# Products with diagonals of 1/rms for turning x, and changed orders and buffers around four stages of a decoder block

## The chip, the cores and the metric

The kernel runs on one core of a Trainium2 chip. The metric is the device time of one execution in microseconds (us), as the median of several runs.

## What is computed

The reference is a decoder block over 1024 positions with 1024 channels, all in float32. Its core is

```python
mod = einsum('bd,de->be', silu(c), w_ada) + b_ada
sh1, sc1, g1, sh2, sc2, g2 = split(mod, 6)
h = rmsnorm(x, norm1_g) * (1 + sc1) + sh1
cb, cc, cv, q, k, v, f_logit, ga, gb = split(h @ w_in, IN_OFFSETS)
ya = cb * causal_dwconv(cc * cv, conv_a_w)
yb = forgetting_attention(rmsnorm(q), rmsnorm(k), v, log_sigmoid(f_logit + b_f))
merged = sigmoid(ga) * (ya @ w_branch_a) + sigmoid(gb) * (yb @ w_branch_b)
x = x + g1 * (merged @ w_out)
h2 = rmsnorm(x, norm2_g) * (1 + sc2) + sh2
gate, val = split(causal_dwconv(h2 @ w_up, conv_ffn_w), 2)      # 2816 channels each
x = x + g2 * ((silu(gate) * val) @ w_down)
```

where `rmsnorm(x, g)` is `x * rsqrt(mean(x*x) + 1e-6) * g`.

## The kernel before

Each float32 operand of a large product is split into a high part and a low part (type fp32r), and a product is the sum of three products of parts. The high part is a copy on ACT, the low part a subtraction on VectorE (DVE) or GpSimd (POOL); `wsplit` (L93, L94) does so for weights. Stages of the network that allow it use Strassen's seven products of blocks in place of eight.

In nearly every stage the order of the instructions on each engine is written out by hand: an engine runs them in the order of the code, and a semaphore wait holds up all that stands behind it on the same engine. The stages are these, by the profile's clock.

- **Head and K pass**, 0 to 78 us. x comes in eight tiles `xts[j]` of 128 positions by 1024 channels. `x_square` sums the squares of a tile on DVE (L292) or ACT (L290), `x_scale` takes the root and multiplies the tile in place by 1/rms (L299), `x_turn` transposes it on PE in two groups of four 128x128 blocks (L306), each copied by ACT into `raw` (L312). Meanwhile rows of the small vectors (`rc` for c, `rv` for gains and biases) are loaded and turned, and the modulation vector is summed: `ada_mul` and `ada_chain` multiply loaded weight blocks `wa` by columns of silu(c) and add them up on DVE, `ada_sum` sums over partitions by a product with ones (L249). `h_tile` applies shift and scale and splits h into parts; `k_mm` makes the K projection, one of eight blocks `dd` of channels at a time, for all tokens. Per odd `dd` the next unit of weights is split.
- **V pass**, 78 to 143 us, and **q pass**, 143 to 201 us. One token (128 positions) after the other is projected. An event table `at(t, f)` hangs the other work on units of PE's work of some 0.7 us each: the norm of the queries (L496 the sums of squares, L501 the normalised queries `qn`, L509 their transposes, L516 and L519 their parts), further blocks of the modulation vector (`rest_mul`: L460 and L463 on DVE, L461 and L464 on ACT, L465 and L467 on POOL), and 16 sums of blocks of h for a later Strassen stage (`t_sum`, L585).
- **Convolution and gates** 201 to 460 us, **attention** 460 to 700, **branches and output projection** 700 to 800.
- **Up-projection**, 800 to 1200 us. The first three units `u0`, `u1`, `u2` are plain products (`plain(n, half)`, n being one of four blocks of a gate or a value); from `U[3]` on it is Strassen. Each unit is scaled, goes through the taps of its convolution and is multiplied out (`scale_g`, `scale_v`, `taps_g`, `silu`, `taps_v`, `ff`, `ff_out`). The Strassen units need sums of blocks of h2 in parts; the sum `T4` (L1481, L1487, made by `t_op(kk, 3, ...)`) is written over the block `B12`, which the plain units still read.
- **Down-projection**, 1200 to 1458 us: seven Strassen products, each over 11 steps of `st.mm(banks)` (L1984). When a product is done, `x_add` adds it to the output blocks (L2009), and finished blocks are turned back: `x_turn_out` has four transposes on PE into the product's own bank (L2020), a copy on ACT (L2026) and a store. One product finishes two blocks, so that two such turns use the same bank.

Of the kernel before, what the change touches and what calls it, by code (L numbers as in the profile page):

```python
# [8 lines left out]
F32 = mybir.dt.float32  # L9
F32R = mybir.dt.float32r  # L10
AF = mybir.ActivationFunctionType
ALU = mybir.AluOpType
# [4 lines left out]
P = 128  # L17
S = 1024
D = 1024
# [14 lines left out]
def tile_hybrid_block(  # L34
# [27 lines left out]
    mm = tensor.matmul  # L62
# [154 lines left out]
    def ada_mul(wa, ks=range(ND), acc=None):  # L217


        acc = acc or [ap.tile([P, 2, P], F32, tag=f"wacc{i}", name="wacc", bufs=1) for i in range(2)]  # L220
        for k in ks:
            a, src = acc[k % 2], wa[:, :, k, :]
            if k < 2:
                vector.tensor_scalar(out=a, in0=src, scalar1=cT[:, k : k + 1], scalar2=None, op0=ALU.mult)
            else:
                vector.scalar_tensor_tensor(out=a, in0=src, scalar=cT[:, k : k + 1], in1=a, op0=ALU.mult, op1=ALU.add)
        if k < ND - 1:
            return acc
        vector.tensor_tensor(out=acc[0], in0=acc[0], in1=acc[1], op=ALU.add)
        return acc[0]  # L230

    def ada_chain(wa, part):

        sums = hT[:, 256:512].rearrange("p (i m) -> p i m", i=2)
        for k in range(4 * part, 4 * part + 4):
            src, c1 = wa[:, :, k, :], cT[:, k : k + 1]
            if k == 0:
                vector.tensor_scalar(out=sums, in0=src, scalar1=c1, scalar2=None, op0=ALU.mult)
                continue
            out = sums  # L240
            if k == ND - 1:
                out = ap.tile([P, 2, P], F32, tag="wacc0", name="wacc", bufs=1)
            vector.scalar_tensor_tensor(out=out, in0=src, scalar=c1, in1=sums, op0=ALU.mult, op1=ALU.add)
        return out

# [42 lines left out]
    def x_square(j, eng):  # L288
        if eng is scalar:
            scalar.activation(accs[2 if j > 3 else 0], xts[j], AF.Square, accum_out=ms[:, j : j + 1])  # L290
        else:
            vector.tensor_tensor_reduce(out=accs[2 if j > 3 else 1], in0=xts[j], in1=xts[j], scale=1.0, scalar=0.0,  # L292
                                        op0=ALU.mult, op1=ALU.add, accum_out=ms[:, j : j + 1])

    def x_scale(j, eng):
        js = slice(j, j + 1)
        vector.tensor_scalar(out=ms2[:, js], in0=ms[:, js], scalar1=1.0 / D, scalar2=EPS, op0=ALU.mult, op1=ALU.add)
        r = newton_rsqrt(xp, ms2[:, js], 1, "r1", root_of=(ms[:, js], 1.0 / D))
        eng.tensor_scalar(out=xts[j], in0=xts[j], scalar1=r, scalar2=0.0, op0=ALU.mult, op1=ALU.add)  # L299

    def x_turn(j, eng=scalar):
        for i in range(2):
            pt = aux_tile("xTp", ("aux", "aux2")[i])
            for n in range(4):
                dd = 4 * i + n
                tensor.transpose(pt[:, n * P : (n + 1) * P], xts[j][:, dd * P : (dd + 1) * P], ident)  # L306
            dst = raw[i, j // 4][:, :, (j % 4) * P : (j % 4 + 1) * P]
            src = pt.rearrange("p (a b) -> p a b", a=4)
            if i and eng is vector:
                vector.tensor_copy(dst, src)  # L310
            else:
                scalar.activation(dst, src, AF.Copy)  # L312
# [29 lines left out]

    scalar.activation(cT, rows_T(c_rows, "rc"), AF.Silu)
    x_square(0, vector)
    x_square(1, vector)
    x_scale(0, gpsimd)
    x_square(2, scalar)
    x_scale(1, vector)
    x_square(3, scalar)
    x_scale(2, gpsimd)  # L350
    x_turn(0)
    x_scale(3, vector)
    x_turn(1)
    vector.tensor_copy(vT[:, :76], rows_T(v_rows, "rv"))
    n1g, n2g = vT[:, 0:8], vT[:, 8:16]
    caw = vT[:, 16:28].rearrange("p (t n) -> p t n", t=3)
# [1 line left out]

    a1b = cp.tile([P, ND], F32, name="a1b")
    vector.scalar_tensor_tensor(out=a1b, in0=bada[:, 8:16], scalar=1.0, in1=n1g, op0=ALU.add, op1=ALU.mult)  # L360
    wc[0] = ada_mul(was[0])
    h_ada(3)
    x_turn(2)
    x_turn(3)
    units[0] = wsplit(kraw[0], gpsimd)
    h_mod(0, ada_sum(wc[0], aux_tile("pm")))
    h_tile(0, 0)
    for j in (4, 5):
        x_square(j, vector)
    for j in (4, 5):  # L370
        x_scale(j, gpsimd)
    for j in (6, 7):
        x_square(j, scalar)
    for j in (6, 7):
        x_scale(j, vector)
    k_mm(0, range(4))
    for j in range(4, NT):
        x_turn(j)
    acc0.append(aux_tile("k6", "aux2"))
# [9 lines left out]
    wc[2] = ada_chain(was[2], 1)  # L389
    h_ada(5)  # L390
    h_tile(1, 1)
    units[1] = wsplit(kraw[1], gpsimd)
    kraw[2] = unit_fetch(O_K, 512, 2)
    vraw = []
    for dd in range(1, ND):
        if dd == 2:
            kraw[3] = unit_fetch(O_K, 512, 3)
        if dd > 4:
            vraw.append(unit_fetch(O_V, 520, dd - 5))
        if dd == ND - 1:  # L400
            for j in range(7):
                for t in TERMS:
                    k_mm(dd, (j,), (t,))
            break
        k_mm(dd, range(7), TERMS[:1])
        if dd % 2:
            units[dd // 2 + 1] = wsplit(kraw[dd // 2 + 1], gpsimd)
        h_mod(dd + 1, ada_sum(wc[dd + 1], hT))
        if dd + 2 < ND:
            ada_chain(was[dd + 2], 0)  # L410
        h_tile(dd + 1, 0)
        if dd + 2 < ND:
            wc[dd + 2] = ada_chain(was[dd + 2], 1)
        if dd + 5 < ND:
            h_ada(dd + 5)
        h_tile(dd + 1, 1)
        k_mm(dd, range(7), TERMS[1:])
# [31 lines left out]
    def rest_mul(part):  # L449
# [2 lines left out]
            return  # L452
        b, wa = rest_open[0]
        if part == 0:
            rest_acc[:] = [ap.tile([P, 2, P], F32, tag=f"wacc{i}", name="wacc", bufs=1) for i in range(2)]
        even, odd = rest_acc
        k = 2 * part
        src, nxt = wa[:, :, k, :], wa[:, :, k + 1, :]
# [85 lines left out]
    def at(t, *fs):  # L544
        events.setdefault(t, []).extend(fs)
# [35 lines left out]

    def sub(o, a, b):
        gpsimd.tensor_tensor(out=o, in0=a, in1=b, op=ALU.subtract)  # L585

    def t_sum():

        kk, n = divmod(t_done.pop(0), 4)
        b11, b12, b21, b22 = (raw[i, g][:, kk] for i in range(2) for g in range(2))  # L590
        sub(*((b11, b12, b11), (b12, b22, b12), (b22, b22, b11), (b21, b21, b22))[n])

    t_done = list(range(16))

# [314 lines left out]
    at(TQ + 19, f_sum)  # L909
    at(TQ + 34, f_turn)  # L910
    for i in range(9):
        at(TQ + 8 * (i // 2) + (1, 3)[i % 2], t_sum)
    for i in range(4):
        at(TQ + (42, 45, 50, 53)[i], lambda i=i: t_split(T1, 0, 0, i, (vector, gpsimd)[i % 2]))
    at(TQ + 55, p0)
# [906 lines left out]
            U[3].fetch(up)  # L1822
    u2.xs = wsp[4:6]
    u2.g, u2.v = (acc4(nm) for nm in ("upg", "upv"))
    for n in (0, 2, 1, 3):
        for half in range(2):
            u2.plain(n, half)
    for kk in range(NK):
        t_op(kk, 3, False)
        t_op(kk, 3, True)  # L1830
    u1.scale_g()
    u1.scale_v()
    u1.taps_g()
    u1.silu()
    U[3].x_split()
    u1.taps_v()
    u1.ff()
    u1.ff_out()
# [211 lines left out]
    for t, st in enumerate(steps[: len(steps) - NE + 1]):  # L2050
# [28 lines left out]
            steps[t + 2].split()  # L2079
        for w in ends.get(t, ()):  # L2080
            w()
        while turns:
            x_turn_out(*turns.pop(0))
        if st.c > 0 and adds and (st.c % 2 == 0 or st.p == ORDER[-1]):
            adds.pop(0)()
        if t < len(steps) - NE:
            st.mm(banks)
    last = steps[-NE:]

    def finish(e):  # L2090
# [47 lines left out]
```

## Time and profile before

| | |
|---|---|
| time, three runs (us) | 1464.48, 1466.3, 1464.09; median 1464.48 |
| the profiled execution (us) | 1460.0 |
| its span, first to last instruction (us) | 1458.3 |
| mean granted clock of TensorE | 0.993 |
| PE busy | 1399.7 us, 96% |
| PE's weight loads (PEld) busy | 1154.3 us, 79% |
| DVE busy | 1086.3 us, 74% |
| ACT busy | 661.9 us, 45% |
| POOL busy | 515.2 us, 35% |

The profile is of one execution. PE stands for the matrix products, PEld for the loads of their stationary operand, which overlap them. Idle time of an engine is put down to the instruction on another engine, or the transfer, that ended it. Matmul ends are modelled, so PE's busy share is an upper bound. The granted clock is a share of full speed.

### The profile page before, as it was taken

To read this page: it belongs to the slowest core of one execution; us is meant where nothing else is said; L and a number is where in the kernel's file an instruction comes from. 1 tells how busy PE (TensorE), PEld (TensorE's weight loads), DVE (VectorE), ACT (ScalarE), POOL (GpSimd) and SP (SyncE) were. 2 spreads that over 40 slices of the span, in tenths; PEclk is the share of its full clock that TensorE was granted. 3 is DMA by queue.
4 is the path that set the end of the run, shared out by engine and by line. 5 is a ranking of instruction groups with operands and counts; after the bars stand their busy time and mean duration, and the time that the engine had idled before them with its cause. 6 is when DMAs were issued, how large, how long until landed. Compare 5 with 4: busy or idle time off the path is not lost. (4 is left out here: it accounts for less than half of the span.)

```text
span 1458.3 us, 19429 instructions
## 1 busy us (share of the span) xinstructions
PE 1399.7 (96%) x6680; PEld 1154.3 (79%) x6680; DVE 1086.3 (74%) x1779; ACT 661.9 (45%) x1147; POOL 515.2 (35%) x540
## 2 busy tenths in 40 slices
PE   5899899999999999999999989999999999999997
PEld 4688678887888888777788868888888887888876
DVE  7865588888777776448637867888887776898764
ACT  6554263434555555565225434544443334444443
POOL 2656457764555553323121013455543321000000
PEclk9999999999999999999999999999999999999999
DMA  9559434546555548676942223344322204983622
GB/s 287 164 165 312 131 101 118 158 110 202 152 145 144 145 123 280 219 258 230 201 131 73 72 69 103 89 116 116 101 87 88 87 29 143 388 290 104 215 77 78
DMA packets 260760, 222.45 MB, mean 153 GB/s; under 512 B 43117, under 2 KB 213445, under 8 KB 260661
## 3 DMA queue, kind: packets, MB, share of 16 engines
q1 hardware_dynamic: 259389, 218.61, 50.2%
q0 software_dynamic: 1136, 2.56, 0.6%
q8 instruction: 53, 0.87, 0.3%
q14 instruction: 46, 0.38, 0.1%
q10 hardware_dynamic: 136, 0.04, 0.0%
HBM read 169.76 MB, written 51.41 MB: 152 GB/s over the span
## 5 line engine op out<-in xcount | busy, mean ns | idle before, releaser
L1984 PE MATMUL dn<-bH,aH 128*128 128x512 f32 x308 | 120.9, 392 | 0.0
L1984 PE MATMUL dn<-bL,aH 128*128 128x512 f32 x308 | 120.2, 390 | 0.6 <-DVE bL L1978 0.6
L1984 PE MATMUL dn<-bH,aL 128*128 128x512 f32 x308 | 119.9, 389 | 0.0
L1594 ACT ACTIVATE wh<-ws 128x512 fp32r<-128x512 f32 x95 | 55.5, 626 | 119.8 <-POOL ws L1628 117.0
L753 DVE TENSOR_TENSOR ol<-ws,oh 128x512 fp32r<-128x512 f32 x98 | 92.5, 952 | 15.0 <-ACT oh L752 11.7
L94 DVE TENSOR_TENSOR wl<-ws,wh 128x1024 fp32r<-128x1024 f32 (+1 forms) x51 | 70.2, 1377 | 36.8 <-ACT wh L93 36.7
L752 ACT ACTIVATE oh<-ws 128x512 fp32r<-128x512 f32 x98 | 61.3, 627 | 70.7 <-PE pacc L798 36.9
L1628 POOL TENSOR_TENSOR ws<-ws 128x512 f32<-128x512 f32 x19 | 24.7, 1299 | 147.0 <-DVE wl L94 147.0
L1595 DVE TENSOR_TENSOR wl<-ws,wh 128x512 fp32r<-128x512 f32 x76 | 69.6, 935 | 8.9 <-ACT wh L1594 8.9
L1195 ACT ACTIVATE L<-L,mn 128x256 f32<-128x256 f32 (+6 forms) x56 | 46.4, 829 | 58.1 <-DVE mn L1193 56.6
L1198 POOL TENSOR_SCALAR L<-L,rs 128x384 f32<-128x384 f32 (+7 forms) x62 | 48.1, 776 | 68.4 <-DVE rs L1197 66.7
L1218 ACT ACTIVATE th<-pt 128x512 fp32r<-128x512 f32 (+1 forms) x80 | 43.9, 551 | 56.2 <-PE pt L1212 53.8
L1984 PEld LDWEIGHTS dn<-bL,aH 128*128 128x128 f32 x308 | 57.9, 188 | 13.2 <-DVE bL L1978 1.5
L585 POOL TENSOR_TENSOR ws<-ws 128x512 f32<-128x512 f32 x42 | 55.0, 1309 | 37.4 <-DVE ol L753 25.4
L1977 ACT ACTIVATE aH<-dws 128x512 fp32r<-128x512 f32 x52 | 32.8, 631 | 76.6 <-issue 44.1
L1984 PEld LDWEIGHTS dn<-bH,aH 128*128 128x128 f32 x308 | 57.8, 188 | 12.1 <-ACT bH L1977 0.4
L1984 PEld LDWEIGHTS dn<-bH,aL 128*128 128x128 f32 x308 | 57.8, 188 | 12.0
L93 ACT ACTIVATE wh<-ws 128x1024 fp32r<-128x1024 f32 (+1 forms) x58 | 60.9, 1052 | 11.2 <-PE k L556 3.1
L1219 DVE TENSOR_TENSOR tl<-pt,th 128x512 fp32r<-128x512 f32 (+1 forms) x80 | 50.5, 635 | 17.4 <-ACT th L1218 15.8
L1715 DVE SCALAR_TENSOR_TENSOR u<-upv,cwT,u 128x1023 f32<-128x1023 f32 (+1 forms) x44 | 56.4, 1281 | 9.5 <-ACT u L1711 8.8
L1595 POOL TENSOR_TENSOR wl<-ws,wh 128x512 fp32r<-128x512 f32 x19 | 24.6, 1297 | 109.3 <-ACT wh L1594 109.3
L1978 DVE TENSOR_TENSOR aL<-dws,aH 128x512 fp32r<-128x512 f32 x52 | 35.9, 691 | 36.3 <-ACT aH L1977 36.3
(571 smaller groups left out, 4523.1 us busy)
## 6 DMA issues: line engine op xcount, KB each, us to landing
wa<-in_w_ada_dram SPq DMA_DIRECT2D x48, 512.0 KB
dws<-in_w_down_dram SPq DMA_DIRECT2D x96, 256.0 KB
ws<-in_w_up_dram SPq DMA_DIRECT2D x44, 512.0 KB
ws<-in_w_in_dram SPq DMA_DIRECT2D x36, 512.0 KB
ff<-ff_d SPq DMA_DIRECT2D x44, 256.0 KB
ff_d<-u SPq DMA_DIRECT2D x21, 512.0 KB
xt<-in_x_dram SPq DMA_DIRECT2D x8, 512.0 KB
v_d<-vt SPq DMA_DIRECT2D x8, 512.0 KB
```

Of the source, the lines that this page charges most:

```text
L93: scalar.activation(wh[:, : n * m], ws[:, : n * m], AF.Copy)
L94: eng.tensor_tensor(out=wl[:, : n * m], in0=ws[:, : n * m], in1=f32(wh[:, : n * m]), op=ALU.subtract)
L585: gpsimd.tensor_tensor(out=o, in0=a, in1=b, op=ALU.subtract)
L752: scalar.activation(h, src, AF.Copy)
L753: eng.tensor_tensor(out=l, in0=src, in1=f32(h), op=ALU.subtract)
L1195: scalar.activation(L[:, :n], L[:, :n], AF.Exp, scale=-1.0, bias=mn, accum_out=sm)
L1198: eng.tensor_scalar(out=L[:, :n], in0=L[:, :n], scalar1=rs, scalar2=0.0, op0=ALU.mult, op1=ALU.add)
L1219: vector.tensor_tensor(out=flat[2][:, c0:], in0=flat[0][:, c0:], in1=f32(flat[1][:, c0:]), op=ALU.subtract)
L1594: scalar.activation(ops[0][:, sl], src, AF.Copy)
L1595: eng.tensor_tensor(out=ops[1][:, sl], in0=src, in1=f32(ops[0][:, sl]), op=ALU.subtract)
L1715: vector.scalar_tensor_tensor(out=u[:, s:], in0=acc[:, : S - s], scalar=cwT[:, 2 - s, n : n + 1], in1=u[:, s:], op0=ALU.mult, op1=ALU.add)
L1984: mm(banks[e], self.A[i][:, es_], self.B[j], start=self.p in FIRST and self.c == 0 and t == 0, stop=self.c == NC - 1 and t == 2, skip_grou ...
```

## The change

The roots are taken for two tiles at a time on DVE (`x_root`), which also makes for each tile a diagonal matrix of 1/rms, and `x_turn` multiplies each block of x by that diagonal in a plain float32 product in place of transposing a scaled block; `x_scale` is gone. The order of the head is rewritten around that: the small vectors' turn and copy come ahead of the second square, and the second four tiles' squares and roots come behind the first part of the K products. The low parts of the K weights move from POOL to DVE. The two accumulators of the modulation sums become one name with two buffers, and the odd sum is made in place in the loaded weights. Nine of the T sums of the q pass move from POOL to DVE. In the up-projection `u2`'s products have another order and T4's splits come behind `U[3].x_split()`. In the down-projection the second of two turns in one bank is placed between the two halves of the next step's products.

```diff
-        acc = acc or [ap.tile([P, 2, P], F32, tag=f"wacc{i}", name="wacc", bufs=1) for i in range(2)]
+        acc = acc or [ap.tile([P, 2, P], F32, tag="wacc", name="wacc", bufs=2), wa[:, :, 1, :]]
...
-                out = ap.tile([P, 2, P], F32, tag="wacc0", name="wacc", bufs=1)
+                out = ap.tile([P, 2, P], F32, tag="wacc", name="wacc", bufs=2)
...
-    def x_scale(j, eng):
-        js = slice(j, j + 1)
+    diags = {}
+    def x_root(j0):
+        js = slice(j0, j0 + 2)
         vector.tensor_scalar(out=ms2[:, js], in0=ms[:, js], scalar1=1.0 / D, scalar2=EPS, op0=ALU.mult, op1=ALU.add)
-        r = newton_rsqrt(xp, ms2[:, js], 1, "r1", root_of=(ms[:, js], 1.0 / D))
-        eng.tensor_scalar(out=xts[j], in0=xts[j], scalar1=r, scalar2=0.0, op0=ALU.mult, op1=ALU.add)
+        r = newton_rsqrt(xp, ms2[:, js], 2, "r1", root_of=(ms[:, js], 1.0 / D))
+        for i in range(2):
+            diags[j0 + i] = xp.tile([P, P], F32, tag="dg", name="dg", bufs=4)
+            vector.tensor_scalar(out=diags[j0 + i], in0=ident, scalar1=r[:, i : i + 1], scalar2=None, op0=ALU.mult)
...
-                tensor.transpose(pt[:, n * P : (n + 1) * P], xts[j][:, dd * P : (dd + 1) * P], ident)
+                mm(pt[:, n * P : (n + 1) * P], xts[j][:, dd * P : (dd + 1) * P], diags[j], start=True, stop=True)
...
     x_square(0, vector)
-    x_square(1, vector)
-    x_scale(0, gpsimd)
-    x_square(2, scalar)
-    x_scale(1, vector)
-    x_square(3, scalar)
-    x_scale(2, gpsimd)
-    x_turn(0)
-    x_scale(3, vector)
-    x_turn(1)
     vector.tensor_copy(vT[:, :76], rows_T(v_rows, "rv"))
...
+    x_square(1, vector)
+    x_root(0)
+    x_square(2, scalar)
+    x_square(3, scalar)
+    x_root(2)
+    x_turn(0)
+    x_turn(1)
     wc[0] = ada_mul(was[0])
     h_ada(3)
     x_turn(2)
+    units[0] = wsplit(kraw[0], vector)
     x_turn(3)
-    units[0] = wsplit(kraw[0], gpsimd)
     h_mod(0, ada_sum(wc[0], aux_tile("pm")))
     h_tile(0, 0)
-    for j in (4, 5):
-        x_square(j, vector)
-    for j in (4, 5):
-        x_scale(j, gpsimd)
-    for j in (6, 7):
-        x_square(j, scalar)
-    for j in (6, 7):
-        x_scale(j, vector)
     k_mm(0, range(4))
+    x_square(4, vector)
+    x_square(5, vector)
+    x_root(4)
+    x_square(6, scalar)
+    x_square(7, scalar)
+    x_root(6)
...
-    units[1] = wsplit(kraw[1], gpsimd)
+    units[1] = wsplit(kraw[1])
...
-            units[dd // 2 + 1] = wsplit(kraw[dd // 2 + 1], gpsimd)
+            units[dd // 2 + 1] = wsplit(kraw[dd // 2 + 1])
...
-            rest_acc[:] = [ap.tile([P, 2, P], F32, tag=f"wacc{i}", name="wacc", bufs=1) for i in range(2)]
+            rest_acc[:] = [ap.tile([P, 2, P], F32, tag="wacc", name="wacc", bufs=2), wa[:, :, 1, :]]
...
     for i in range(9):
-        at(TQ + 8 * (i // 2) + (1, 3)[i % 2], t_sum)
+        at(TQ + 8 * (i // 2) + (1, 3)[i % 2], lambda: t_sum(vector))
...
-    for n in (0, 2, 1, 3):
-        for half in range(2):
-            u2.plain(n, half)
-    for kk in range(NK):
-        t_op(kk, 3, False)
-        t_op(kk, 3, True)
+    for n, half in ((0, 1), (1, 1), (0, 0), (2, 0), (2, 1), (1, 0), (3, 0), (3, 1)):
+        u2.plain(n, half)
     u1.scale_g()
     u1.scale_v()
     u1.taps_g()
     u1.silu()
     U[3].x_split()
+    for kk in range(NK):
+        t_op(kk, 3, False)
+        t_op(kk, 3, True)
...
-        while turns:
-            x_turn_out(*turns.pop(0))
+        first, second = turns[:1], turns[1:]
+        turns.clear()
+        for a in first:
+            x_turn_out(*a)
         if st.c > 0 and adds and (st.c % 2 == 0 or st.p == ORDER[-1]):
             adds.pop(0)()
-        if t < len(steps) - NE:
-            st.mm(banks)
+        st_es = (range(2), range(2, 4)) if second else (range(4),)
+        for n, es in enumerate(st_es):
+            if n:
+                x_turn_out(*second[0])
+            if t < len(steps) - NE:
+                st.mm(banks, es)
```

## Rows read from the trace of the kernel before

**Rows 1.** Waits over the span: who waits for whom, us in total, times, longest.
```profile
PE qT L509 <- DVE qn L501: 7.2, 2, 5.7
...
PE dn L2020 <- ACT ot L2026: 4.3, 4, 1.1
PE hT L249 <- DVE wacc L243: 4.1, 4, 1.1
...
PE qacc L556 <- DVE wl L94: 1.5, 1, 1.5
...
PE qT L509 <- DVE ql L519: 1.1, 2, 0.9
```

**Rows 2.** Timeline of PE, head: start, duration (us), instructions, [idle before, releaser].
```profile
9.49 1.57 PEld L306 LDWEIGHTS xTp<-ident,xt 128*128 128x128 f32 x8 [6.41 <-POOL xt L299]
...
28.02 1.15 PE L306 MATMUL xTp<-ident,xt 128*128 128x128 f32 x8 [0.25 <-ACT raw L312]
...
29.36 1.15 PE L306 MATMUL xTp<-ident,xt 128*128 128x128 f32 x8 [0.20 <-ACT raw L312]
```

**Rows 3.** Timeline of DVE and POOL, head.
```profile
5.89 1.23 DVE L292 CUSTOM_DVE_ANT_0 k<-xt 128x1024 f32<-128x1024 f32 x1
...
8.32 1.12 POOL L299 TENSOR_SCALAR xt<-xt,r1r 128x1024 f32<-128x1024 f32 x1 [6.80 <-DVE ms L297]
```

**Rows 4.** Waits of SP's queue in the first 12 us.
```profile
SPq L80 <- DMA rv<-in_norm_g_dram: 0.5, 1, 0.5
```

**Rows 5.** Timeline of PE, DVE and POOL in the K pass.
```profile
45.09 0.60 PE L249 MATMUL hT<-ones,wacc 128*128 128x1 f32 x4 [1.04 <-DVE wacc L243]
45.22 0.69 DVE L329 TENSOR_TENSOR h01L<-raw,h01H 128x512 fp32r<-128x512 f32 x1 [0.20 <-POOL raw L328]
...
50.03 2.42 POOL L94 TENSOR_TENSOR wl<-ws,wh 128x1024 fp32r<-128x1024 f32 x1
50.40 2.61 DVE L329 TENSOR_TENSOR h01L<-raw,h01H 128x512 fp32r<-128x512 f32 x1
50.54 0.60 PE L249 MATMUL hT<-ones,wacc 128*128 128x1 f32 x4
...
57.19 0.61 PE L249 MATMUL hT<-ones,wacc 128*128 128x1 f32 x4 [1.07 <-DVE wacc L243]
```

**Rows 6.** Timeline of DVE in the up-projection.
```profile
831.55 1.22 DVE L94 TENSOR_TENSOR wl<-ws,wh 128x1024 fp32r<-128x1024 f32 x1
```

**Rows 7.** Timeline of the engines in the q pass.
```profile
155.23 0.51 ACT L461 ACTIVATE wacc<-wa,cT 128x256 f32<-128x256 f32 x1 [4.97 <-DMA wa<-in_w_ada_dram]
...
159.37 0.52 DVE L460 TENSOR_SCALAR wacc<-wa,cT 128x256 f32<-128x256 f32 x1 [5.41 <-PE pm L249]
...
162.30 5.31 POOL L585 TENSOR_TENSOR raw<-raw,raw 128x512 f32<-128x512 f32 x4
...
167.17 1.09 PE L509 MATMUL qT<-ident,qn 128*128 128x128 f32 x4 [5.70 <-DVE qn L501]
```

**Rows 8.** Windows: length, busy time of PE, PEld, DVE, ACT, POOL, granted clock, DMA share, GB/s.
```profile
167.10:171.30 4.20, 4.13 (x14) 3.47 (x15) 1.34 (x3) 1.18 (x2) 0.52 (x1) 0.50 0.33 93
854.00:874.00 20.00, 16.08 (x64) 11.52 (x64) 16.73 (x16) 8.34 (x12) 6.45 (x5) 1.00 0.27 82
1417.50:1437.10 19.60, 15.30 (x82) 12.23 (x81) 10.33 (x17) 8.93 (x16) 0.00 (x0) 1.00 0.37 105
```

**Rows 9.** Timeline of ACT in the up-projection.
```profile
846.54 2.73 ACT L1481 ACTIVATE T4H<-x 128x512 fp32r<-128x512 f32 x4 [19.12 <-PE upv L1604]
```

**Rows 10.** Timeline of PE in the down-projection.
```profile
1417.58 0.64 PE L2020 MATMUL dn<-ident,xo 128*128 128x128 f32 x4
...
1419.29 0.66 PE L2020 MATMUL dn<-ident,xo 128*128 128x128 f32 x4 [1.08 <-ACT ot L2026]
```

**Rows 11.** Timeline of PE around products of plain float32, output projection.
```profile
767.04 1.05 PE L1472 MATMUL pb<-U,ones 128*128 128x128 f32 x8
767.85 0.48 PE L108 MATMUL mix<-mH,wh 128*128 128x512 f32 x1
```

More of the change, by code (lines that the diff above doesn't have):

```diff
@@ L574, in hook, with sub, t_sum @@
         return out
-    def sub(o, a, b):
-        gpsimd.tensor_tensor(out=o, in0=a, in1=b, op=ALU.subtract)
-    def t_sum():
+    def sub(o, a, b, eng=gpsimd):
+        eng.tensor_tensor(out=o, in0=a, in1=b, op=ALU.subtract)
+    def t_sum(eng=gpsimd):
         kk, n = divmod(t_done.pop(0), 4)
         b11, b12, b21, b22 = (raw[i, g][:, kk] for i in range(2) for g in range(2))
-        sub(*((b11, b12, b11), (b12, b22, b12), (b22, b22, b11), (b21, b21, b22))[n])
+        sub(*((b11, b12, b11), (b12, b22, b12), (b22, b22, b11), (b21, b21, b22))[n], eng)
     t_done = list(range(16))
```

## The prediction

> **What bounds the kernel now.** I read the page first. PE is busy for 1399.7 of 1458.3 us, and every other engine has a quarter of the span or more to spare. So an edit gains only where it closes a hole in PE's work or shortens what PE does. The second view is the list of PE's waits over the span [rows 1]. It is short, and most of its entries lie where the diff works: 7.2 us for the normalised queries of the q pass, 4.3 us for the copies ahead of the output transposes, 4.1 us for the sums of the modulation vector in the K pass, and 1.5 and 1.1 us at the borders of the V and q passes. The third view is the timeline around each. In the head [rows 2, 3] PE stands still until tile 0 is scaled on POOL, and the second four turns of x come every 1.34 us (28.02 to 29.36), each waiting 0.2 us for ACT's copy. In the K pass [rows 5] the modulation sums follow each other after 5.45 us (45.09 to 50.54) and then after 6.65 us (50.54 to 57.19). In the q pass [rows 7] four things stand in a line: ACT's first product waits 4.97 us for a load; VectorE's waits 5.41 us for a buffer that PE still reads; four subtractions on POOL run from 162.30 to 167.61; PE waits 5.70 us, to 167.17. The last view is windows [rows 8]: after that wait the granted clock is 0.50 for 4.2 us (the lower of the two levels, 1.2 GHz); in the 20 us from 854 PE is busy for 16.08 us; in the 19.6 us near the end for 15.30 us. In the last two the clock is full, so these are plain holes.
>
> **The change part by part.** All terms are us on the profiled span of 1458.3; its execution took 1460.0, and the median of the runs shown, 1464.48, is 4.5 above that. I apply the sum to the median.
>
> *q pass.* The even accumulator had one buffer, and its first write had to wait until PE had read the old one (159.37). Behind it in VectorE's order stand the sums of squares, the root and the normalised queries that PE waits for. With two buffers under one name that write needs only the loaded weights, which had arrived by 155.23. The nine T sums at these places leave POOL. There they take 1.3 us each (5.31 for four); on VectorE I price them at the 0.69 of a 512-wide subtraction [rows 5]. Up to two of them then stand ahead of the same chain, 1.4 us, but VectorE regains the 5.41 us. Counting its operations forward from 155.7 I get the normalised queries some 0.7 us after PE wants them. What is late next is the load: ACT's 4.97 us for it are unchanged. Gain of the wait 5.70 - 0.7 = 5.0. The slow stretch goes with the hole: 4.2 us at half clock hold 2.1 us of work at full clock, so 2.1 more. Together **-7.1**; bounds -7.8 (no wait left) and -4.9 (2.9 us left, all the chain late). The waits of 1.1 (queries' low parts) and 1.5 us (a weight split that POOL's T sum holds up) at the pass's borders [rows 1] go in part, since their causes are the same: I take 0.9 and 0.7, **-1.6**, bounds 0 and -2.6.
>
> *Up-projection.* ACT waits 19.12 us, to 846.54, to overwrite operands that PE still multiplies [rows 9], and all of the next units' scaling, taps and splits stand behind it. They come late, and PE shows 20 - 16.08 = 3.92 us of holes from 854 on. The new order uses those operands' last readers up earlier, and puts the overwrite behind the work that was late. I take the whole hole, **-3.9**; bounds -3.5 (the first split still late by 0.4) and -4.9 (the ends of products are modelled, so a busy PE may hide a quarter more).
>
> *Tail.* Two turns in one bank: the second group of transposes overwrites the bank, so it waits for the copy of the first. The groups start 1.71 us apart [rows 10], 1.08 of that idle, four times over. Half the step's products between them (six) cover at least 6 x 0.19 = 1.1 us by the mean of the window (15.30 over 82), which is more than the wait. **-4.3**; bounds -4.0 (the wait shrinks to under 0.1 each) and -4.6 (1.71 less four transposes at 0.14 [rows 2], four times).
>
> *K pass.* While POOL makes a low part for 2.42 us, the 0.69 us subtraction on VectorE takes 2.61: it loses 1.92. If VectorE makes the low part it pays 1.22 [rows 6] and loses none. That is 0.7 us better in each of two odd steps; the first odd step splits twice and loses about 0.4. **-1.0**; bounds 0 and -2.4 (both odd steps become as short as even ones, 1.2 each). The odd accumulators made in place free nothing here; they hold the weights' buffer longer, whose next load has the time of a whole step.
>
> *Head.* The scalings (1.12 us on POOL, less on VectorE) go; in their place come two roots of two tiles each before the first turn, two diagonals a root, and products. The chain before the first turn now holds the small vectors' transposes and copy (SP's wait shows their load landing just before 6 us [rows 4]), then the second square, 1.23, then root and diagonal. Before, 2.4 us lay from the start of square 1 to the scaling (5.89 to 8.32), and 1.17 more to the first turn. I allow 1.5 us for the load, PE's transposes and the copy: square 1 now starts near 7.4, ends near 8.6, the root ends near 11, two diagonals and the start bring 12.0 instead of 9.49: +2.5. A product with a diagonal is no transpose: the nearest rows are L1472's four calls [rows 11], each 128 columns of plain fp32, with two records a call, 0.81 us for all, so 0.20 each. Eight make 1.6 and with the copy's handover 1.78 a turn, against 1.34 at present: +0.44 for each of the four late turns, 1.7. In the first four turns PE has gaps now, and there I cost the products at nothing, hidden by ACT's copies and VectorE's roots. The first product over K follows these turns at once and should regain about 1.1 that it loses now on late tiles. **+3.1**; bounds -0.5 (the first turns start earlier than I think and all else is hidden) and +8 (all eight turns at the pace of the first loads, 1.57 / 8 = 0.196 for each of 16, 3.14 a turn: +5 beyond my term).
>
> The Trainium skill speaks against this edit (TensorE: Matmul & The Clock Gate, Terms): on trn2 a transpose mode makes FP32 transposes four times faster, so a product would cost four transposes. The trace does not agree: 0.20 us for a product against 1.15 / 8 = 0.14 for a transpose. By the rule the head would cost 22.6 us more, and the sum would be a loss of 7.8.
>
> Sum: -7.1 - 1.6 - 3.9 - 4.3 - 1.0 + 3.1 = **-14.8**, 1464.5 - 14.8 = 1449.7.
>
> **The rivals.**
>
> *Head dear.* All turns run at the slow pace; for it speaks that the first loads do [rows 2], against it that the late ones don't. +8 in place of +3.1: -9.9, 1454.6.
>
> *The q pass keeps its hole.* The load lands later, or VectorE, which now has the T sums, is late itself. For it: ACT's 4.97 us on the load; against it: that load is there 4 us before VectorE's write. If only 3 of the 7.1 come: -10.7, 1453.8.
>
> *The late scaling still waits.* In the up-projection the scaling's target may not be free, and the hole moves: -10.9, 1453.6.
>
> *Other side: a product costs four transposes.* Place: all eight turns, in the head, where PE has nothing else to do. Four times 1.15 is 4.60 a turn, 2.82 above my 1.78, 22.6 for eight: +7.8, 1472.3. It decides from (14.8 / 8 =) 1.85 us a turn above my price, 3.6 us a turn. Against it stands L1472's 0.20; for it, that no row here shows a product of this kind straight after idle.
>
> **How the numbers follow.** Forecast as worked out, within 4 us of it: 0.62. Head dear 0.16, q pass 0.12, late scaling 0.04, the other side 0.04; 0.02 that several gains fail and the time stays. The likeliest gives 1449.5. The low end takes the better bounds of q pass, borders and tail (-0.7 - 1.0 - 0.3) and the head at -0.5, 1444, with 1 below for what I didn't see: 1443. The high end takes in each of the first three rivals alone, and two of them half: 1457. A measurement of this kernel can tell about 0.2% (2.9 us) from no change: faster by more 0.94, within 0.02, slower 0.04.
>
> **What would show it.** Right: first turn near 12 us and late turns 1.8 us apart, with two matmul records a call; VectorE's L460 with no wait for PE, PE's wait for the queries under 1 us and a full clock after it; no T sum of x on POOL before the last seven; ACT's T4 split without its 19 us wait and PE full in the stretch from 854; the four waits for the output copies gone; odd steps of the K pass near 6 us. Wrong: turns of 3 us and more, a first turn after 15 us, a new wait of PE for VectorE in the q pass (its T sums named as releaser), or holes that come back one stage later in the up-projection.

## The result and the profile after

The changed kernel takes 1452.86 us (median, 1449.52 to 1453.91) against 1464.28 us before: a ratio of 0.9927, 95% interval 0.9902 to 0.9951, or 11.4 us less. Measured again beside other kernels it took 1449.23 us, a ratio of 0.9912 (0.9897 to 0.9928). The forecast was 1449.5 (1449.7 by its own sum), with a range of 1443 to 1457.

The profiled execution took 1452.13 us, its span 1450.2, which is 8.1 below the span before. The medians lie 3.3 further apart, because the execution profiled before was a quick one of its kernel (1460.0, median 1464.28). The line of busy time on the page (us, share of the span, instructions): PE works 7 us longer in a span that is 8 us shorter (3 us longer in the second profile).

```profile
PE 1406.7 (97%) x6744; PEld 1165.3 (80%) x6744; DVE 1084.9 (75%) x1777; ACT 660.9 (46%) x1143; POOL 487.0 (34%) x522
```

To see where the time went, I took the starts of the same PE instructions in each trace and list the stretches between them (us). "Twice" is the changed kernel's second profile; the last two columns are experiments below.

| stretch, by PE's first instruction at its end | before | changed | twice | head back | head back, turns apart |
|---|---|---|---|---|---|
| start to K product over the second half of positions | 31.89 | 38.72 | 37.63 | 32.00 | 31.88 |
| to the first V product | 52.07 | 50.47 | 51.49 | 51.01 | 50.98 |
| to V products over `h11` (a middle token) | 32.37 | 31.88 | 31.97 | 31.97 | 31.89 |
| to q products over `h00` (behind the q pass's hole) | 59.00 | 53.61 | 53.26 | 53.48 | 52.50 |
| to convolution products over `h01` | 40.14 | 41.68 | 41.50 | 40.16 | 41.44 |
| to the first product of the up-projection | 569.02 | 568.86 | 566.83 | 567.15 | 566.64 |
| to the first of the down-projection | 443.15 | 437.35 | 437.34 | 437.35 | 437.34 |
| to the first output transposes | 130.70 | 131.02 | 131.54 | 130.68 | 131.46 |
| to the end | 99.96 | 96.61 | 96.64 | 97.50 | 95.07 |

Each experiment below leaves most stretches alone, so their profiles show how far a stretch moves with its code unchanged: the first from 36.3 to 38.7 us with the changed head, the K pass from 50.4 to 51.5, the one over the q pass from 52.5 to 55.3, the one with attention from 566.6 to 572.3, the last from 96.6 to 97.5. The one to the convolution takes 40.2 us or some 41.5; the up-projection's moves by 0.02 at most. Of the kernel before there is one profile.

**Head.** The timeline of PE after; [rows 2] has the one before.

```profile
8.27 0.36 PE L201 MATMUL rvp<-ident,rv 76*128 76x76 f32 x1 [5.69 <-DMA rv<-in_b_ada_dram]
13.21 10.01 PE L312 MATMUL xTp<-dg,xt 128*128 128x128 f32 x64 [4.59 <-DVE dg L304]
...
29.84 7.49 PE L312 MATMUL xTp<-dg,xt 128*128 128x128 f32 x64
38.72 0.97 PE L346 MATMUL k<-wh,h01H 128*128 128x512 f32 x3 [1.39 <-ACT h01H L329]
```

The first turn starts at 13.21 in place of 9.49. The first four turns take 10.0 us and the second four 7.5, with 64 records each: two for each of 32 products. The timelines of VectorE and ACT show why the first turn is late; [rows 3] has VectorE's place before.

```profile
8.66 0.24 DVE L351 COPY vT<-rvp 128x76 f32<-128x76 f32 x1 [2.91 <-PE rvp L201]
...
9.02 1.23 DVE L292 CUSTOM_DVE_ANT_0 k<-xt 128x1024 f32<-128x1024 f32 x1
...
12.01 0.17 DVE L173 RECIPROCAL r1y<-r1s 128x2 f32<-128x2 f32 x1 [1.50 <-ACT r1s L170]
```

```profile
10.38 1.28 ACT L170 ACT_TABLE_LOAD   x1 [6.07 <-DVE ms L292]
```

The second square starts at 9.02 (5.89 before), since VectorE's copy waits 2.91 us for the small vectors; and ACT loads the table for the root at 10.38, when nothing else is left to run beside it.

**q pass.** The hole of [rows 7] is closed: the even sum that stood at 159.37 waits for no engine, and starts 0.4 us behind ACT's first product, which still waits for the load. PE's transposes of the queries follow without a wait.

```profile
160.31 0.51 ACT L463 ACTIVATE wa<-wa,cT 128x256 f32<-128x256 f32 x1 [3.26 <-DMA wa<-in_w_ada_dram]
...
160.69 0.83 DVE L462 TENSOR_SCALAR wacc<-wa,cT 128x256 f32<-128x256 f32 x1
...
168.46 0.63 PE L511 MATMUL qT<-ident,qn 128*128 128x128 f32 x4
```

At the border of V and q pass PE's waits have grown from 1.5 us [rows 1] to 2.8 (2.5 in the second profile). The list of PE's waits from 140 to 155 us:

```profile
PE qacc L558 <- ACT wh L93: 1.4, 1, 1.4
PE qacc L558 <- DVE wl L94: 0.8, 1, 0.8
PE qacc L558 <- POOL wl L94: 0.6, 1, 0.6
```

The windows that answer to the first two of [rows 8], with two more (columns as there):

```profile
150.00:155.00 5.00, 3.90 (x9) 2.92 (x10) 3.15 (x8) 3.39 (x6) 0.00 (x0) 0.66 1.07 287
160.00:172.00 12.00, 12.00 (x68) 10.11 (x67) 11.04 (x23) 5.65 (x10) 4.12 (x5) 1.00 0.44 117
208.50:214.50 6.00, 5.95 (x20) 4.58 (x21) 3.60 (x7) 4.19 (x8) 3.48 (x3) 0.72 0.28 63
851.00:871.00 20.00, 20.00 (x89) 16.38 (x88) 14.00 (x16) 6.32 (x9) 6.31 (x5) 1.00 0.43 131
```

PE is full at a full clock from 160 to 172, and full from 851 to 871. Two stretches have a lower clock that they did not have before: behind the border's waits (0.66), and from 208.5 (0.72), where PE waits 2.06 us for queries (2.07 before).

**Up-projection and tail.** ACT's splits of T4 [rows 9] come without a wait; the four waits for the output copies [rows 10] are gone from the list of waits, and two for VectorE's addition are new.

```profile
841.01 2.18 ACT L1483 ACTIVATE T4H<-x 128x512 fp32r<-128x512 f32 x4
```

```profile
PE dn L2021 <- DVE xo L2010: 1.3, 2, 0.7
```

### The profile page after: what moved, and what is told of

The parts are those of the page before. It is cut to its first block, busy times and chain, and to the rows that moved or that the text cites. A ratio compares the mean times of both kernels' runs of the same rounds, so it can differ in the third digit from the quotient of the medians.

```text
span 1450.2 us, 19527 instructions
## 1 busy us (share of the span) xinstructions
PE 1406.7 (97%) x6744; PEld 1165.3 (80%) x6744; DVE 1084.9 (75%) x1777; ACT 660.9 (46%) x1143; POOL 487.0 (34%) x522
## 5 line engine op out<-in xcount | busy, mean ns | idle before, releaser
L94 DVE TENSOR_TENSOR wl<-ws,wh 128x1024 fp32r<-128x1024 f32 (+1 forms) x56 | 75.4, 1349 | 42.4 <-ACT wh L93 42.0
L1221 DVE TENSOR_TENSOR tl<-pt,th 128x512 fp32r<-128x512 f32 (+1 forms) x80 | 50.3, 634 | 18.1 <-ACT th L1220 16.8
```

The source lines that it names most:

```text
L94: eng.tensor_tensor(out=wl[:, : n * m], in0=ws[:, : n * m], in1=f32(wh[:, : n * m]), op=ALU.subtract)
L1221: vector.tensor_tensor(out=flat[2][:, c0:], in0=flat[0][:, c0:], in1=f32(flat[1][:, c0:]), op=ALU.subtract)
```

## The experiments

The theory after this reading: four parts gain what they were meant to (buffers, T4's order, the turns apart, the K units' low parts), and the head, with its products and its order, gives a good part of it back.

**The head as before.** The only edit: `x_root`, the products and the new order of the head are replaced by the removed lines of the diff.

```diff
-                mm(pt[:, n * P : (n + 1) * P], xts[j][:, dd * P : (dd + 1) * P], diags[j], start=True, stop=True)
+                tensor.transpose(pt[:, n * P : (n + 1) * P], xts[j][:, dd * P : (dd + 1) * P], ident)
...
-    x_root(0)
+    x_scale(0, gpsimd)
```

> The changed kernel with the head alone as before the change (a root for each tile, x scaled in place, transposes, the old order); all else stays changed. Theory: the new head costs the whole 6.8 us by which the first product over K's second block of positions starts later (31.89 before, 38.72 after), so that product starts at 31.9 +- 0.5 here and the time is 5 to 7 us below the changed kernel's, 1446 to 1448. Rival: the K pass behind the head has slack (1.6 of the 6.8 us were already back at the start of the V pass), so that most of the lateness is absorbed: the start of the V pass moves by 3 us or less from 89.2 and the time by under 3 us, 1450 to 1453.

It took 1444.76 us (ratio 0.9882, 0.9865 to 0.9899), the lowest median of all: 8.1 us below the changed kernel's first measurement and 4.5 below its second. The first product over the second half of positions starts at 32.00 and the V pass at 83.01, 6.2 us ahead of the changed kernel (and 3.8 to 6.2 ahead of all six profiles that keep its head): nearly all of the head's price lasts, and the rival is out.

**The small vectors late.**

```diff
     x_square(0, vector)
-    vector.tensor_copy(vT[:, :76], rows_T(v_rows, "rv"))
     x_square(1, vector)
...
     x_turn(1)
+    vector.tensor_copy(vT[:, :76], rows_T(v_rows, "rv"))
```

> The changed kernel with one thing in the head undone: the small vectors' transposes and copy stand behind the second turn of x again, no longer ahead of the second square. Theory: of the head's 6.8 us, 3.7 come from the later first turn, and those from the place of these vectors: VectorE waited 2.9 us for them with the second square, the root and ACT's table load behind it. The first turn then starts near 10.1 us (13.21 in the changed kernel) and the time falls by 2 to 3.5 us against the changed kernel's, to 1449 to 1451. Rival: the roots by twos are what is late (two squares before the first root, table load behind them): the first turn stays after 12 us and the time within 1 us of the changed kernel's.

The first turn starts at 10.08 and the V pass at 85.39, 3.8 us ahead of the changed kernel, so the place of these vectors is what makes the first turn late. The other profiles bear it out: in all six with the changed head the first turn starts between 12.51 and 13.45, and each time 4.9 to 5.0 us behind PE's turn of the vectors, which waits for their load. But the V pass starts at 86.8 to 89.2 in these six, so of its lead 1.4 us are clear. The time does not show it: 1450.87 us, between the two measurements of the changed kernel. The lead was lost before the up-projection: PE waits 2.48 us for POOL's low part at the border to the q pass, and the stretch with attention took 2.4 us more in this profile, within what it moves by itself. The line from the list of PE's waits between 138 and 152 us of this kernel:

```profile
PE qacc L558 <- POOL wl L94: 2.5, 1, 2.5
```

So the head's lateness by the first turn is shown, what it is worth in time is not.

**Scaled and transposed, in the new order.**

```diff
-            diags[j0 + i] = xp.tile([P, P], F32, tag="dg", name="dg", bufs=4)
-            vector.tensor_scalar(out=diags[j0 + i], in0=ident, scalar1=r[:, i : i + 1], scalar2=None, op0=ALU.mult)
+            (gpsimd, vector)[i].tensor_scalar(out=xts[j0 + i], in0=xts[j0 + i], scalar1=r[:, i : i + 1], ...)
...
-                mm(pt[:, n * P : (n + 1) * P], xts[j][:, dd * P : (dd + 1) * P], diags[j], start=True, stop=True)
+                tensor.transpose(pt[:, n * P : (n + 1) * P], xts[j][:, dd * P : (dd + 1) * P], ident)
```

> The changed kernel's order and roots by twos, but each tile of x is scaled in place (one of a pair on POOL, one on VectorE) and transposed, in place of products with diagonals. Theory: the products' own price is the difference: the second four turns take 1.35 us each instead of 1.87 (2.1 us in all), the first four 2.0 or less instead of 2.5, less 0.6 us for a scaling that is slower than two diagonals; together the start of the first product over K's second block moves from 38.7 to 35 to 36.5. Rival of four transposes a product (the forecast's other side): the late turns were 4.6 us each in the changed kernel; they are 1.87 there, so this rival is already out, and what is left of it is a price of 2 transposes at most. Rival: the order, not the product, makes the head dear: the start stays at 38 or later.

The timeline of PE in this kernel:

```profile
14.70 6.98 PE L313 MATMUL xTp<-ident,xt 128*128 128x128 f32 x32 [5.96 <-POOL xt L304]
...
30.72 1.14 PE L313 MATMUL xTp<-ident,xt 128*128 128x128 f32 x8 [0.25 <-ACT raw L319]
...
32.16 1.07 PE L313 MATMUL xTp<-ident,xt 128*128 128x128 f32 x8 [0.29 <-ACT raw L319]
...
36.01 0.96 PE L347 MATMUL k<-wh,h01H 128*128 128x512 f32 x3 [1.39 <-ACT h01H L330]
```

The late turns come every 1.4 us, as before the change, and wait for ACT; the first four take 7.0 us instead of 10.0. Although the first turn starts 1.5 us later (scaling takes longer than two diagonals), the product over the second half starts at 36.01, 2.7 us ahead of the changed kernel and within what the theory gave. So both count, but their shares are known only roughly: the six profiles with the changed head have that product at 36.3 to 38.7, so the net gain here lies between 0.3 and 2.7 us. What is steady is the price of the products in the late turns: from their start to the product behind them it takes 6.6 us here, and 8.9 to 9.0 in each of the six. The first four turns take 9.1 to 10.4 us in these, against 7.0. The time, 1449.85 us (1445.45 to 1453.28), is too wide to tell it from the changed kernel's.

**T sums on POOL again.**

```diff
-        at(TQ + 8 * (i // 2) + (1, 3)[i % 2], lambda: t_sum(vector))
+        at(TQ + 8 * (i // 2) + (1, 3)[i % 2], t_sum)
```

> The changed kernel with the nine T sums of the q pass back on POOL; the two sum buffers stay. Theory: the second buffer alone removes the wait of 5.41 us on VectorE and with it PE's 5.7 us; the T sums' engine is worth little, under 1.5 us either way, and no wait of PE for the queries over 1 us comes back. Rival: POOL's four sums in a row hold up VectorE (its operations of 0.2 us took 1 us beside them before), and without the move a wait of 2 to 4 us stays, with a slow stretch of the clock behind it: 3 to 6 us slower than the changed kernel.

1450.81 us: no slower, as the theory had it. But a wait of PE for the queries of 2.0 us is back, twice what the theory allowed, and the stretch over the q pass takes 54.7 us (53.6 and 53.3 changed).

```profile
PE qT L511 <- DVE qn L503: 2.0, 1, 2.0
```

Neither can be put down to the T sums: seven of the other kernels here keep them on VectorE and leave the q pass alone, and in these PE waits 0.8 to 2.5 us at this place, and the stretch takes up to 55.3. The clock stays full behind this wait, so the rival's 3 to 6 us don't come. What the move of the T sums is worth is not shown.

**One buffer for each sum.** The three lines on `acc`, `out` and `rest_acc` as before, among them

```diff
-            rest_acc[:] = [ap.tile([P, 2, P], F32, tag="wacc", name="wacc", bufs=2), wa[:, :, 1, :]]
+            rest_acc[:] = [ap.tile([P, 2, P], F32, tag=f"wacc{i}", name="wacc", bufs=1) for i in range(2)]
```

> The changed kernel with the two sum accumulators as before (one buffer each under its own name, the odd one not in the loaded weights); the T sums stay on VectorE. Theory: the second buffer is what took the q pass's hole away, so VectorE's wait for PE (5.4 us) and PE's wait for the queries (4 us or more) come back, with a stretch of granted clock near 0.5 behind them: the first product of the next token group (174.68 in the changed kernel, 175.33 before) starts 3 to 7 us later than in the changed kernel, and the time is 3 to 7 us above it. The users of the loaded weights wait less for their load (8 us in all before, 19 changed), because VectorE's wait hides it again. Rival: the T sums' move did it, and the hole stays away: within 1.5 us of the changed kernel.

1458.99 us (ratio 0.9970, 0.9956 to 0.9984): 6.1 above the changed kernel's first measurement, 9.8 above its second. VectorE's first product of a sum waits 4.16 us for PE again, PE 4.56 us for the queries, and the clock behind it is at its lower level. Three views of this kernel: VectorE's and PE's timeline, and a window.

```profile
162.77 0.54 DVE L462 TENSOR_SCALAR wacc<-wa,cT 128x256 f32<-128x256 f32 x1 [4.16 <-PE pm L249]
```

```profile
169.43 1.08 PE L511 MATMUL qT<-ident,qn 128*128 128x128 f32 x4 [4.56 <-DVE qn L503]
```

```profile
169.00:174.00 5.00, 4.57 (x15) 3.91 (x16) 2.90 (x6) 1.21 (x3) 0.00 (x0) 0.50 0.37 103
```

The stretch over the q pass takes 57.6 us, 4.0 more than in the changed kernel and 2.3 more than the longest of the profiles with two buffers. The second buffer closed the hole; the T sums' move alone leaves it.

This run shows one thing more. PE's list of waits from 140 to 155 us has a single entry here, where the changed kernel had 2.8 us in three:

```profile
PE qacc L558 <- DVE wl L94: 0.8, 1, 0.8
```

In the ten profiles with the new accumulators the border's waits for the q weights come to 2.0 to 3.0 us. The users of the loaded modulation weights wait 11.5 us for their loads from 105 to 165 us, 19.1 in the changed kernel. Why the loads are late there stands in the list of the waits of the queue that issues them, of the changed kernel in the same stretch:

```profile
SPq L214 <- POOL wacc L469: 7.1, 2, 4.8
```

L469 is POOL's addition of the odd sum, which now lies in the weights' buffer, to the even one: the next load into that buffer waits for it. With separate accumulators this wait is not in the list.

**T4 in the old order.**

```diff
-    for n, half in ((0, 1), (1, 1), (0, 0), (2, 0), (2, 1), (1, 0), (3, 0), (3, 1)):
-        u2.plain(n, half)
+    for n in (0, 2, 1, 3):
+        for half in range(2):
+            u2.plain(n, half)
+    for kk in range(NK):
+        t_op(kk, 3, False)
+        t_op(kk, 3, True)
```

> The changed kernel with the third unit's products and T4's splits in the old order. Theory: ACT's wait of 19 us and PE's holes of 3.9 to 4.9 us in the 20 us behind the third unit come back, and the time is 4 to 5 us above the changed kernel's. Rival: with the rest of the kernel changed the stage takes another course (other transfers beside it), and the order is worth under 2 us.

1458.19 us, 5.3 above the changed kernel's first measurement and 9.0 above its second. The wait and the holes are back, in ACT's timeline and in the window:

```profile
845.88 1.33 ACT L1483 ACTIVATE T4H<-x 128x512 fp32r<-128x512 f32 x2 [19.13 <-PE upv L1606]
```

```profile
853.00:873.00 20.00, 16.05 (x65) 11.34 (x64) 16.38 (x16) 8.68 (x12) 6.47 (x5) 1.00 0.26 76
```

The up-projection's stretch takes 443.2 us, as before the change, against 437.35 in every profile with the new order: 5.8 us for this part.

**Both turns of a bank at once.** The end of the step as before the change (`while turns: x_turn_out(*turns.pop(0))`, then `st.mm(banks)`).

> The changed kernel with both turns of a bank ahead of the next step's products again. Theory: the four waits of 1.1 us for ACT's copy come back (4.3 us) and the two new waits of 0.65 us for VectorE's addition go, so the stretch from the first output transposes to the end is 3.0 to 3.6 us longer and the time 3.0 to 3.6 us above the changed kernel's. Rival: the new waits stay (they come from the order of the additions, not from the split), and the difference is the full 4.3 to 5.

1456.31 us, 3.4 above the changed kernel's first measurement and 7.1 above its second, so the size is read from the profile: the last stretch takes 99.9 us as before (96.6 changed), as the theory had it. PE's list of waits has the four for the output copies again, and none for VectorE's addition:

```profile
PE dn L2021 <- ACT ot L2027: 4.3, 4, 1.1
```

**No low part on POOL at the border.**

```diff
-            dst.append(wsplit(raws.pop(0), (vector, gpsimd, vector, vector)[u]))
+            dst.append(wsplit(raws.pop(0), vector))
```

> The changed kernel, with the low part of the second V unit and the second q unit made by VectorE, no longer by POOL. The waits at the border of V and q pass, 1.5 us before the change, are 2.7 us after it (0.6 for POOL's low part, which takes 3.3 us beside VectorE's, 0.8 for VectorE's, 1.4 for ACT's high part). Theory: POOL and VectorE slow each other there as they did in the K pass; with both low parts on VectorE at 1.2 us each the border's waits fall to under 1.5 us and the time by 1 to 2.5 us. Rival: the weights' loads set the border, and the waits only change their releaser: within 1 us.

1452.27 us, the same as the changed kernel: the rival's time. Its trace spans 5816.7 us and can't be set beside the others, so which waits took the others' place is not known.

**The head back and the turns further apart.** The first experiment's kernel, and in the down-projection

```diff
+        if todo and live:
+            st.mm(banks, (next(es),))
+        if todo:
+            x_turn_out(*todo[0])
...
+        if len(todo) > 1:
+            if live:
+                st.mm(banks, (next(es), next(es)))
+            x_turn_out(*todo[1])
```

> The head as before the change, all else changed, and in the down-projection the first turn of a bank stands behind the first quarter of the next step's products, the second behind three quarters. Theory: the head gives 7 to 9 us against the changed kernel, as it did alone (1444.8), and the two new waits of 0.65 us for VectorE's addition go, 1.3 to 1.7 us: 1443 to 1444, and the last stretch without a wait of PE over 0.4 us. Rival: the additions are late at any place, the waits move behind the first quarter: no better than the head alone, 1444.8 or above.

1444.94 us (ratio 0.9877, 0.9858 to 0.9896). In the profile the two waits for VectorE's addition are down to 0.10 and 0.13 us and the last stretch takes 95.1 us, 1.5 less than in the changed kernel. In the time it can't be told from the head alone (1444.76). These two are the best versions here, both below the changed kernel.

**K units' low parts on POOL again.** `units[...] = wsplit(..., gpsimd)` at all three places.

> The changed kernel with the low parts of the K units back on POOL. Theory: VectorE's subtractions beside POOL's low parts take 2.6 us again in place of 0.7, the odd steps of the K pass grow from 6.0 to 6.6 us, and the pass, from the first product over the second block to the start of the V pass (50.5 us in the changed kernel, 52.1 before), takes 0.7 to 1.7 us more. The time is about 1 us above the changed kernel's, within what can be told. Rival: the move is worth nothing, the pass keeps 50.5 within 0.3 us, and its 1.6 us came from the sums' buffers.

1452.34 us, 3.1 above the changed kernel in the same comparison, with intervals that overlap (0.9918 to 0.9951 against 0.9897 to 0.9928). The K pass takes 51.9 us, 0.4 to 1.5 more than in the profiles with all low parts on VectorE (50.4 to 51.5), and VectorE's subtraction beside POOL's low part 2.6 again. The slow subtraction is shown; what it is worth in the pass is known only this roughly. The groups of VectorE in that stage of this kernel (instruction, count, busy us, mean ns, idle before):

```profile
L335 DVE TENSOR_TENSOR h01L<-raw,h01H 128x512 fp32r<-128x512 f32 x4 | 6.6, 1648 | 6.1 <-POOL raw L334 6.1
```

and the same group of the changed kernel:

```profile
L335 DVE TENSOR_TENSOR h01L<-raw,h01H 128x512 fp32r<-128x512 f32 x4 | 2.7, 687 | 5.2 <-POOL raw L334 5.2
```

**The changed kernel again.**

> The changed kernel itself, unchanged, on the same chip as the two kernels beside it, so that they stand against it directly: 1450 to 1454, a ratio of 0.992 to 0.994 to the kernel before. If its head, its first turn at 13.2 us and its border of V and q pass come out as in its first profile, those lie in the code; if they move by more than 1 us, that much of the accounts of single profiles is chance.

1449.23 us. The first turn starts at 13.28 and the border's waits are 0.5, 1.2 and 0.8 us: by the rule set out ahead of the run, both lie in the code. Three things move by 1 us and more between the two profiles: the first product over K (the granted clock from 25.5 to 29.84 us is 0.63 in the first and 1.00 in the second, and the second four turns start at 29.84 and 28.65), the K pass (PE waits 2.6 us for the sums of the modulation vector, 1.4 in the first), and the stretch with attention.

## Why the prediction held, and where it was off

Direction and range held. Of the rivals, "head dear" came half true: the first four turns ran at 2.5 us each, the late ones did not, and the head's +6.8 lies nearer to that rival's +8 than to +3.1. The others did not come. The terms against the stretches of the table, on profiled spans, with the second profile in brackets:

| term | forecast | measured |
|---|---|---|
| head | +3.1 | +6.8 (+5.7) |
| K pass | -1.0 | -1.6 (-0.6) |
| V and q pass with their borders | -8.7 | -5.9 (-6.1) |
| behind the q pass | 0 | +1.5 (+1.4) |
| T4 | -3.9 | -5.8 (-5.8) |
| tail | -4.3 | -3.35 (-3.3) |
| the other stretches | 0 | +0.2 (-1.3) |
| sum | -14.8 | -8.1 (-10.1) |

So each mechanism came, but the sum on spans was 6.7 too good, and 4.7 by the second profile. That the medians (11.4 and 13.4 us less) lie nearer to -14.8 is partly luck: the one execution profiled before was quicker than its kernel's median, and the terms' errors go both ways.

**Head: the step that was off most.** "In the first four turns PE has gaps now, and there I cost the products at nothing" did not hold. With the later start nothing is left to hide behind: PE is busy in all of the 10.0 us, and from the first turn to the products with ones 10.3 us pass, 8.2 before: +2.0 for a term of 0. The first turn came 1.2 us later still than I worked out (+3.7 for +2.5): VectorE waited 2.91 us for the vectors, and the table load stood in the open behind the second square. I read the landing of the vectors from SP's wait of 0.5 us [rows 4], but that is another part of them: PE's wait names the load of the last biases, near 8.2 us. The other two steps were nearer. The late turns cost 7.5 / 4 = 1.87 us each for 1.78, so the price from L1472 [rows 11] carried over, and from their start to the product behind them it takes 2.3 us more than before (1.7 forecast); the first product over K won back 1.2 (1.1 forecast). Undoing the head alone took the median to 1444.76, which is 18.1 below the kernel before in its comparison; the other terms of the forecast sum to -17.9; with single terms off by up to 3 us either way, that they agree so closely is luck.

**The rule on transposes.** A turn of eight transposes takes 1.07 to 1.15 us on PE in the kernel that scales and transposes, a turn of eight products 1.87: 1.7 times as long. The Trainium skill (TensorE: Matmul & The Clock Gate, Terms) gives transposes a mode that is four times faster for FP32. By that rule a late turn would have taken some 4.4 us; the measurement decides, and the rival on the other side (from 3.6 us a turn) was far off.

**q pass.** The mechanism was right: the second buffer closed the hole, and the clock stayed full from 160 to 172 us. In place of 0.7 us of waiting there was none in the changed kernel's first profile and 0.13 us in its second, but that was a good draw. "What is late next is the load" held: in the two profiles ACT waits 3.3 and 3.5 us for it; in the seven other kernels with this q pass the load is later, VectorE's even sum waits 0.5 to 2.0 us for it too, and PE waits 0.8 to 2.5 for the queries.

The terms at the borders failed: of -1.6, the V pass gave -0.5 and the border to the q pass grew worse. PE stands there 2.8 us in place of 1.5, with a stretch at a granted clock of 0.66 behind it. The prediction had said of the K pass that sums made in place hold the weights' buffer longer, and had not carried this over to the V and q passes. There it delays the next loads (7.1 us of waits of the issuing queue for POOL's last addition), and the instructions on these weights wait 19.1 us for them, 8.3 before. That the accumulators are the cause is shown, in one profile: with the old ones the border's waits are 0.8 us. How a late load comes to hold up PE is argued from the order of the work: ACT, which makes the high parts of the q weights, waits for the load ahead of them. That the in-place sum alone does it, without the second buffer, was not run.

**Clock behind the q pass.** PE waits 2.06 us (2.07 before) for queries near 208 us, but in the changed kernel the granted clock fell behind that wait (0.72 over 6 us), which costs the 1.5 us. In the twelve profiles with that stretch the clock fell there in five and not in seven, behind waits of 2.06 to 2.10 us. All five are of kernels with parts of the change, but so are six of the seven, so nothing ties it to the change.

**T4 and tail.** T4's whole delay was in the old order, not only the hole I counted: the stretch became 5.8 us shorter, beyond the bound of 4.9. PE's waits in the window of 20 us come to 3.9 of it, but busy time does not show all that the products lose: 64 began in that window and 89 in the one after, and 25 more at 20 / 89 us each are 5.6 us. In the tail the four waits went (4.3 us of waits, some 5.0 by the starts of the products), and two of 0.65 us came up (some 1.65 by the starts) that were hidden behind them: transposes that now reach VectorE's addition too early. I had priced the cover and not looked at what comes next on VectorE.

**K pass.** VectorE's subtractions beside POOL's low parts were slow for the reason given; that this gave the whole 1.0 is not shown, as the pass moves by as much between profiles. The group's mean is 1648 ns with POOL and 687 without. It agrees with the Trainium skill (SBUF — State Buffer, Who interferes with whom): a VectorE instruction with two inputs in SBUF contends with a GpSimd instruction that reads it.

## What to carry to other kernels

A wait on a buffer that another engine still reads can cost more than its own length: here PE stood 5.70 us behind it and then ran at half clock for 4.2. A second small buffer removed VectorE's wait, and what moving other work beside it gave was too small to tell. A result made in place in a loaded buffer saves room, but it holds that buffer until the result is read, and so the load that comes next. Work put on PE to relieve other engines is only hidden where PE waits after the change as well: count its cover in the new order, from the new start. When a wait is removed, look for the next one on the same engine in both directions of time: here it came up as loads in the block ahead and as additions in the tail. And where one part of a kernel is judged from one profile, look first at how far that part moves in the profiles of kernels that leave it alone.

## Not expected of the hardware

- A product of a 128x128 block with a diagonal in plain float32 leaves two records and costs 0.23 us (7.49 us for 32 products) where it follows another; in the first 10.0 us of the changed kernel 0.31, at a granted clock of 1.00 and with transfers at 351 GB/s (the window below). Transposes are slower there too (6.98 us for 32, against 1.1 for eight later). What slows both was not tested.

```profile
13.20:23.20 10.00, 9.98 (x64) 9.82 (x64) 4.99 (x18) 6.06 (x11) 0.00 (x0) 1.00 1.11 351
```

- The granted clock after a wait of PE is not set by the wait's length alone. Behind waits of 2.06 to 2.10 us near 208 us it fell in five profiles (0.72 over 6 us in the changed kernel) and stayed at 1.00 in seven. In the q pass it stayed at 1.00 behind 2.0 us (T sums on POOL) and behind 2.5 us (K units' low parts on POOL), fell behind 1.9 us (both turns of a bank at once; 0.69 from 167 to 172.5 us), and was 0.50 behind 4.56 us.
